# The q and k transposes of the last head group, moved from TensorE to DMAs of 16-bit planes

## Chip, cores and metric

One core of one Trainium2 chip. The metric is the device time of one execution in microseconds (us). TensorE is called PE, VectorE DVE, ScalarE ACT, GpSimd POOL and SyncE SP, as in the rows of the profile.

## What is computed

One decoder layer on 256 tokens of width 2048, all in float32. An RMS norm of x feeds one projection, which gives q, k and v of 16 heads of 128 and three gates. Heads 0 to 3 attend by stick breaking, 4 to 9 by a softmax with a bias by distance, 10 to 15 by a dilated softmax with a bias. q and k of heads 4 to 15 are normalised per row first:

```
proj = h @ w_in
qn = rmsnorm(q[:, H_A:], q_gain[:, None, :])
kn = rmsnorm(k[:, H_A:], k_gain[:, None, :])
l = einsum('bhqd,bhkd->bhqk', qn, kn) * scale + bias      # then a masked softmax, times v
merged = sum over branches of gates * (o_branch @ w_branch)
x = x + merged @ w_out
x = x + (silu(gate(h2)) * up(h2)) @ w_down                # h2: second RMS norm
```

The scores need q and k with the head dimension on the 128 partitions; the projection leaves them with the tokens there. So every 128x128 block of q and k is transposed once.

## The kernel before, in words

**Weights.** Every weight block comes in float32 from SP's DMA queue as 128x1024. ACT rounds it to a high part (`w_hi`, line 108), DVE subtracts to get the low part (`w_lo`, line 108), and PE forms three products of 128x512 for each 128 rows (lines 170 to 172). `parts` does this for one block, with five buffers each for `w_hi` and `w_lo`. Two column blocks at a time go through one Strassen step (`project_pair`), called a unit here. A unit has 22 calls of `parts`, the last four of them ahead for the next unit (`begin_pair`). Sums of two blocks are called `u`.

**Units.** Their order in the first phase is v of group 0, a gate, q and k of groups 0 and 1 (`qk`), v of groups 1 and 2, q and k of groups 2 and 3, then v of group 3 with a gate ("vg"), and five units of two gates each. A group is four heads; group 3 is the last.

**Side work.** Generators hold the work beside the products. `stages` goes one step forward after each weight split, `slow_stages` after every second one. `rows_to_columns(3)` runs in `stages` during the unit "vg": it scales the four 128x512 tiles `sbs` (q of token tiles 0 and 1, k of 0 and 1), takes their sums of squares on ACT (line 729), works out `rr` on DVE and ACT (lines 177 to 186), multiplies each tile by it on DVE (line 739), transposes it on PE in four 128x128 pieces (`transpose4`, line 192), and takes the result out of PSUM: k by an ACT copy (line 745), q by a DVE product with the gains in reversed order (line 748). The attention of group 3 is queued in `slow_stages` after "vg", behind that of group 2.

**What follows "vg" on ACT.** v is scaled out of PSUM (line 798), the gate goes through a sigmoid (line 772, with a load of another function table), then come the splits of the first gate unit and the copies of its partial sums (`snapshot`, line 308), and beside them the softmax of group 2 (line 693, again with a table load).

**Order.** The instructions of each engine are put in order by a planner that plays the program through with its own durations; an instruction written earlier goes first among those that are ready. `keep_in_program_order` only pins an instruction behind the one written before it on its engine. On the chip each engine takes its own list in that order. `half_kb` hands out one of 12 scratch tiles of 128x512.

**The method itself is in the kernel already.** `to_a`, in the feed-forward phase, splits a tile into its 16-bit halves on ACT (line 998), transposes the halves by a DMA issued from ACT (line 1001) and joins them on ACT (line 1008); there the issue is one step behind the split, and the join at least six steps behind the last issue.

Of the kernel before, what the change touches and what calls it, by code (L numbers as in the profile page):

```python
# [11 lines left out]
U16 = mybir.dt.uint16  # L12
# [6 lines left out]
P = 128  # L19
D = 2048  # L20
S = 256
NT = S // P
KT = D // P
HD = 128
H_A, H_B, H_C = 4, 6, 6
# [30 lines left out]
def hybrid_block(ctx: ExitStack, tc: tile.TileContext, x, w_in, w_branch, w_out, w_gu, w_down, rel_bias,  # L56
                 onehot, extra, across, factors, out):
    nc = tc.nc
# [32 lines left out]
    def half_kb(dt=F32):  # L91

        return scratch.tile([P, NB], dt, name="sc")
# [80 lines left out]
    def rsqrt_mean(dst, ss, n, cols):  # L174

        v = small.tile([P, cols], F32, name=f"rs_v{cols}")
        nc.vector.tensor_scalar(v, ss, 1.0 / n, EPS, op0=ALU.mult, op1=ALU.add)
        y = small.tile([P, cols], F32, name=f"rs_y{cols}")
        nc.scalar.activation(y, v, AF.Ln)
        nc.scalar.activation(y, y, AF.Exp, scale=-0.5)  # L180
        t = small.tile([P, cols], F32, name=f"rs_t{cols}")
        for it in range(2):
            nc.vector.tensor_mul(t, y, y)
            nc.vector.tensor_mul(t, t, v)
            nc.vector.tensor_scalar(t, t, -0.5, 1.5, op0=ALU.mult, op1=ALU.add)
            nc.vector.tensor_mul(dst if it else y, y, t)

    def transpose4(src):

        pt = tr.tile([P, 4, P], F32, name="tr")  # L190
        for i in range(4):
            nc.tensor.transpose(pt[:, i, :], src[:, i * P:(i + 1) * P], ident)  # L192
        return pt


    class Columns:

# [203 lines left out]
    h = Columns(p1, "h", KT)  # L401
    hs = Both(p1, h, WC)
# [32 lines left out]
    gq = consts.tile([P, H_SOFT], F32, name="gq")  # L435
# [181 lines left out]
    def backwards(a):  # L617


        return a[..., ::-1]  # L620
# [97 lines left out]
    def rows_to_columns(g, sbs, dst):  # L718
        for i in (0, 2, 3):
            tc.keep_in_program_order(nc.scalar.activation(sbs[i], sbs[i], AF.Copy, scale=rstd[:, i % NT:i % NT + 1]))  # L720
            if i != 2:
                yield
        if g:
            ss = pa.tile([P, 4 * NT * 2], F32, name="ss", bufs=1)
            for i, sb in enumerate(sbs):
                junk = half_kb()
                for hd in range(4):
                    cols = slice(hd * HD, (hd + 1) * HD)
                    tc.keep_in_program_order(nc.scalar.activation(junk[:, cols], sb[:, cols], AF.Square,
                                                                  accum_out=ss[:, 4 * i + hd:4 * i + hd + 1]))  # L730
                    if hd % 2:
                        yield
            rr = pa.tile([P, 4 * NT * 2], F32, name="rr", bufs=1)
            rsqrt_mean(rr, ss, HD, 4 * NT * 2)
            yield
        for i, sb in enumerate(sbs):
            if g:
                sb3 = sb.rearrange("p (h d) -> p h d", h=4)
                nc.vector.tensor_mul(sb3, sb3, rr[:, 4 * i:4 * i + 4, None].to_broadcast([P, 4, HD]))
            yield  # L740
            j, t = divmod(i, NT)
            pt = transpose4(sb)
            d = dst[j][:, :, t * P:(t + 1) * P]
            if j:
                nc.scalar.copy(d, pt)
            elif g:
                hs = 4 * g - H_A
                nc.vector.tensor_mul(d, backwards(pt), gq[:, hs:hs + 4, None].to_broadcast([P, 4, P]))
            else:
                nc.scalar.activation(d, pt, AF.Copy, scale=SCALE)  # L750
        yield

    def attention(g, qT, kT, v):
        biases = []
# [50 lines left out]
    def keep_qk(g, q0, q1, k0, k1):  # L805
        sbs = [q0, half_kb(), k0, k1]
        nc.scalar.activation(sbs[1], q1, AF.Copy, scale=rstd[:, 1:2])
        heads["qk", g] = qkT = [pa.tile([P, 4, S], F32, name=f"{n}T") for n in "qk"]
        if g:
            stages.append(rows_to_columns(g, sbs, qkT))  # L810
        else:
            slow_stages.append(rows_to_columns(g, sbs, qkT))
            attend(g)
# [161 lines left out]
    a = Chunks(None, "a", NF // 4, WD, False)  # L975
# [231 lines left out]
```

## Time and profile before

| | |
|---|---|
| median of 3 runs | 1344.98 us (1343.92 to 1347.02) |
| the profiled execution | 1344.12 us, its span 1342.4 us, 1.7 us outside the span |
| granted clock of PE | 1.00 (2.4 GHz) |
| busy | PE 99%, DVE 86%, ACT 68%, POOL 9% of the span |

A busy share is an average over the whole span. What a change of 20 us in one place is worth is read from that place: the order of time on PE, ACT and DVE there, and the spare time between the end of a weight split and its first product. An ACT row of two or more instructions gives the time from the start of the first to the end of the last; consecutive ones overlap by about 0.1 us.

### The profile page before, as it was taken

The numbers are of one execution on the slowest core, as the hardware profiler recorded it, in microseconds if no ns is written. First come the engines' busy times: TensorE is split into PE (matmuls) and PEld (weight loads), VectorE is DVE, ScalarE is ACT, GpSimd is POOL, SyncE is SP. The second block draws the span as 40 slices with busy tenths as digits, with TensorE's granted clock in tenths as the row PEclk, the third lists the DMA queues.
The fourth block names the chain that finished last, engine by engine and source line by source line (L and its number), as shares of the span: only waits on it lengthen the run. The fifth ranks groups of instructions, "written<-read, shape, count | busy, mean of one in ns | idle before, by whom it ended". The sixth has DMA issues, their size and how long they took to land.

```text
span 1342.4 us, 17715 instructions
## 1 busy us (share of the span) xinstructions
PE 1333.9 (99%) x6266; PEld 1165.2 (87%) x6266; DVE 1154.9 (86%) x1239; ACT 917.4 (68%) x1175; POOL 118.0 (9%) x180
## 2 busy tenths in 40 slices
PE   9999999999999999999999999999999999999998
PEld 6888888888888888888888888888888888888887
DVE  7988898988889996876689999999999997996785
ACT  7786967888776775445567778777877876664453
POOL 1100010101110112100100000001000001000000
PEclk9999999999999999999999999999999999999999
DMA  9987877888788878977788989899999987787652
GB/s 361 305 282 248 268 208 246 269 255 244 250 276 278 268 241 286 309 232 223 238 325 258 269 250 282 222 263 302 289 281 284 245 240 254 251 307 239 204 186 96
DMA packets 117200, 346.83 MB, mean 258 GB/s; under 512 B 32576, under 2 KB 34296, under 8 KB 117112
## 3 DMA queue, kind: packets, MB, share of 16 engines
q1 hardware_dynamic: 76872, 277.45, 59.6%
q0 software_dynamic: 17824, 61.90, 19.7%
q10 hardware_dynamic: 22416, 6.36, 2.8%
q8 instruction: 49, 0.80, 0.2%
q14 instruction: 39, 0.32, 0.1%
HBM read 293.21 MB, written 14.70 MB: 229 GB/s over the span
## 4 chain that ended last, share of the span: by engine, by line
PE 96%; DVE 2%; ACT 1%; issue 0%; DMA 0%; SPq 0%; DVEq 0%; ACTq 0%
PE qs L171 12%; PE qs L170 12%; PE qs L172 12%; PE ps L171 12%; PE ps L172 12%; PE ps L170 12%; PE z L170 4%; PE z L171 4%; PE z L172 4%; PE v L171 2%; PE v L172 2%; PE v L170 2%; PE tr L172 1%; PE tr L170 1%; PE tr L171 1%; PE tr L192 1%
## 5 line engine op out<-in xcount | busy, mean ns | idle before, releaser
L108 DVE TENSOR_TENSOR w_lo<-w_raw,w_hi 128x1024 fp32r<-128x1024 f32 x318 | 386.9, 1221 | 86.2 <-ACT w_hi L108 84.6
L108 ACT CAST w_hi<-w_raw 128x1024 fp32r<-128x1024 f32 x318 | 331.8, 1048 | 142.9 <-PE qs L172 49.3
L108 ACT CAST w_hi<-g_raw 128x1024 fp32r<-128x1024 f32 x200 | 207.5, 1049 | 131.8 <-PE qs L172 37.1
L108 DVE TENSOR_TENSOR w_lo<-g_raw,w_hi 128x1024 fp32r<-128x1024 f32 x200 | 238.7, 1221 | 29.6 <-ACT w_hi L108 28.0
L108 ACT CAST w_hi<-u 128x1024 fp32r<-128x1024 f32 x150 | 155.4, 1047 | 79.7 <-PE ps L172 20.7
L108 DVE TENSOR_TENSOR w_lo<-u,w_hi 128x1024 fp32r<-128x1024 f32 x150 | 180.6, 1221 | 32.9 <-ACT w_hi L108 29.9
L171 PE MATMUL qs<-w_lo,h_hi 128*128 128x512 f32 x348 | 132.7, 381 | 0.0
L172 PE MATMUL qs<-w_hi,h_lo 128*128 128x512 f32 x348 | 132.2, 380 | 0.0
L171 PE MATMUL ps<-w_lo,h_hi 128*128 128x512 f32 x336 | 128.1, 382 | 0.2 <-DVE w_lo L108 0.2
L172 PE MATMUL ps<-w_hi,h_lo 128*128 128x512 f32 x336 | 127.5, 380 | 0.1
L170 PE MATMUL qs<-w_hi,h_hi 128*128 128x512 f32 x348 | 125.0, 382 | 0.0
L170 PE MATMUL ps<-w_hi,h_hi 128*128 128x512 f32 x336 | 121.1, 382 | 0.0
L170 PEld LDWEIGHTS qs<-w_hi,h_hi 128*128 128x128 f32 x348 | 65.9, 189 | 9.4 <-ACT sc L308 0.4
L171 PEld LDWEIGHTS qs<-w_lo,h_hi 128*128 128x128 f32 x348 | 65.9, 189 | 9.1
L172 PEld LDWEIGHTS qs<-w_hi,h_lo 128*128 128x128 f32 x348 | 65.9, 189 | 9.1
L172 PEld LDWEIGHTS ps<-w_hi,h_lo 128*128 128x128 f32 x336 | 63.6, 189 | 9.7 <-DVE h_lo L108 1.1
L171 PEld LDWEIGHTS ps<-w_lo,h_hi 128*128 128x128 f32 x336 | 63.6, 189 | 9.6 <-DVE w_lo L108 1.1
L170 PEld LDWEIGHTS ps<-w_hi,h_hi 128*128 128x128 f32 x336 | 63.4, 190 | 8.9 <-ACT h_hi L108 0.3
L366 POOL DMA_DIRECT2D u<-g_raw x44 | 38.2, 868 | 363.6 <-DVE w_lo L108 252.5
L324 DVE TENSOR_TENSOR u<-g_raw 128x1024 f32<-128x1024 f32 x44 | 53.6, 1220 | 7.7 <-DMA g_raw<-in_w_gu 5.8
L313 DVE TENSOR_TENSOR u<-u,g_raw 128x1024 f32<-128x1024 f32 x44 | 51.8, 1218 | 0.0
L171 PE MATMUL z<-w_lo,h_hi 128*128 128x512 f32 x104 | 39.5, 380 | 0.0
(400 smaller groups left out, 2956.5 us busy)
## 6 DMA issues: line engine op xcount, KB each, us to landing
w_raw<-in_w_in SPq DMA_DIRECT2D x104, 512.0 KB, 6.8
g_raw<-in_w_in SPq DMA_DIRECT2D x88, 512.0 KB, 6.5
g_raw<-in_w_gu SPq DMA_DIRECT2D x88, 512.0 KB, 6.2
w_raw<-in_w_gu SPq DMA_DIRECT2D x88, 512.0 KB, 7.4
w_raw<-in_w_down SPq DMA_DIRECT2D x64, 512.0 KB, 4.3
u<-g_raw POOLq DMA_DIRECT2D x44, 512.0 KB, 6.9
w_raw<-in_w_branch SPq DMA_DIRECT2D x32, 512.0 KB, 4.9
w_raw<-in_w_out SPq DMA_DIRECT2D x32, 512.0 KB, 4.4
```

The source lines that it names most:

```text
L108: for op in nc.scalar.copy(hi, src), nc.vector.tensor_sub(lo, src, hi.bitcast(F32)):
L170: nc.tensor.matmul(ps, ah, wh, start=start, stop=False, **how)
L171: nc.tensor.matmul(ps, ah, wl, start=False, stop=False, **how)
L172: nc.tensor.matmul(ps, al, wh, start=False, stop=stop, **how)
L192: nc.tensor.transpose(pt[:, i, :], src[:, i * P:(i + 1) * P], ident)
L313: tc.keep_in_program_order(nc.vector.tensor_add(d, d, a))
L324: nc.vector.tensor_add(d, a, b)
L366: nc.gpsimd.dma_start(d, a, accum_op=ALU.add)
```

## The change

For group 3 alone the transposes leave PE. After its product with `rr`, each of the four tiles is copied on ACT into a plane of low and a plane of high 16-bit halves (`send_across`), and a DMA issued from ACT writes the transposed planes back over the tile. Three empty steps later ACT joins the halves (`take_across`), one tile a step: k straight into `kT`, q into the tile that held its halves, from which DVE multiplies it by the gains into `qT` (`by_gain`, the old line 748 in a function of its own).

```
+    def send_across(src, turned):
+        halves = half_kb()
+        tc.keep_in_program_order(nc.scalar.copy(halves.bitcast(U16).rearrange("p (h n) -> p h n", h=2),
+                                                src.bitcast(U16).rearrange("p (n h) -> p h n", h=2)))
+        nc.scalar.dma_start_transpose(turned.bitcast(U16).rearrange("p (e q) -> p e q", e=8), halves.bitcast(U16))
+        return halves
+
+    def take_across(dst, turned):
+        tc.keep_in_program_order(nc.scalar.copy(dst, turned.bitcast(U16).rearrange("p (h k q) -> p h k q", h=2, k=4)))
+
+    def words(a):
+        return a.bitcast(U16).rearrange("p (k q h) -> p h k q", k=4, h=2)
...
+        back = []
         for i, sb in enumerate(sbs):
             if g:
                 sb3 = sb.rearrange("p (h d) -> p h d", h=4)
                 nc.vector.tensor_mul(sb3, sb3, rr[:, 4 * i:4 * i + 4, None].to_broadcast([P, 4, HD]))
             yield
+            if g == 3:
+                back.append(send_across(sb, sb))
+                continue
             j, t = divmod(i, NT)
             pt = transpose4(sb)
             d = dst[j][:, :, t * P:(t + 1) * P]
             if j:
                 nc.scalar.copy(d, pt)
             elif g:
-                hs = 4 * g - H_A
-                nc.vector.tensor_mul(d, backwards(pt), gq[:, hs:hs + 4, None].to_broadcast([P, 4, P]))
+                by_gain(d, g, pt)
             else:
                 nc.scalar.activation(d, pt, AF.Copy, scale=SCALE)
-        yield
+        for _ in range(3 if back else 1):
+            yield
+        for i, own in enumerate(back):
+            yield
+            j, t = divmod(i, NT)
+            if j:
+                take_across(dst[j].bitcast(U16).rearrange("p k (q h) -> p h k q", h=2)[:, :, :, t * P:(t + 1) * P], sbs[i])
+            else:
+                take_across(words(own), sbs[i])
+                by_gain(dst[j][:, :, t * P:(t + 1) * P], g, own.rearrange("p (k q) -> p k q", k=4))
+
+    def by_gain(d, g, src):
+        hs = 4 * g - H_A
+        nc.vector.tensor_mul(d, backwards(src), gq[:, hs:hs + 4, None].to_broadcast([P, 4, P]))
```

## Rows read from the trace of the kernel before

**Rows 1.** The page's part 1: busy time of each engine.

```profile
PE 1333.9 (99%) x6266; PEld 1165.2 (87%) x6266; DVE 1154.9 (86%) x1239; ACT 917.4 (68%) x1175; POOL 118.0 (9%) x180
```

**Rows 2.** Waits of PE: total us, times, longest; a row of four.

```profile
PE qs L171 <- DVE w_lo L108: 1.1, 2, 0.8
```

**Rows 3.** The chain that ended last: start us, us, what.

```profile
322.96 0.44 PE tr L192 x4
...
361.24 0.86 PE att L676 x4
```

**Rows 4.** Timeline of ACT after `rr` is known: start us, us, what [idle before].

```profile
305.81 1.05 ACT L108 CAST w_hi<-g_raw 128x1024 fp32r<-128x1024 f32 x1 [1.54 <-PE qs L172]
307.53 0.69 ACT L798 ACTIVATE v<-qs,rstd 128x512 f32<-128x512 f32 x1 [0.68 <-PE qs L172]
308.61 1.05 ACT L108 CAST w_hi<-u 128x1024 fp32r<-128x1024 f32 x1 [0.39 <-DVE sc L739]
...
312.22 1.03 ACT L108 CAST w_hi<-u 128x1024 fp32r<-128x1024 f32 x1
...
314.24 1.05 ACT L108 CAST w_hi<-w_raw 128x1024 fp32r<-128x1024 f32 x1
...
320.16 0.58 ACT L745 COPY kT<-tr 128x512 f32<-128x512 f32 x1
320.63 2.00 ACT L108 CAST w_hi<-u 128x1024 fp32r<-128x1024 f32 x2
```

**Rows 5.** Timeline of DVE in the same stretch.

```profile
306.10 2.49 DVE L739 TENSOR_TENSOR sc<-sc,rr 128x512 f32<-128x512 f32 x4
...
313.28 1.23 DVE L108 TENSOR_TENSOR w_lo<-u,w_hi 128x1024 fp32r<-128x1024 f32 x1 [0.23 <-ACT w_hi L108]
```

**Rows 6.** Timeline of PE: the first products with those splits.

```profile
316.01 0.46 PE L170 MATMUL qs<-w_hi,h_hi 128*128 128x512 f32 x1
316.31 0.38 PE L171 MATMUL qs<-w_lo,b_shi 128*128 128x512 f32 x1
...
323.45 0.38 PE L170 MATMUL ps<-w_hi,b_shi 128*128 128x512 f32 x1
```

**Rows 7.** Busy us and instructions of the engines by stretch.

```profile
316.00:327.00 11.00, 11.00 (x59) 9.48 (x58) 10.03 (x14) 10.97 (x20) 1.79 (x2) 1.00 0.75 226
327.00:348.00 21.00, 21.00 (x106) 18.53 (x105) 17.78 (x20) 12.48 (x16) 0.00 (x0) 1.00 0.77 276
```

**Rows 8.** The tiles `halves` and `turned` of `to_a`: duration ns min/median/max.

```profile
L998 ACT COPY halves<-sc x20: 1043/1045/1058, 733.3 to 1084.8; 128x1024 uint16<-128x1024 uint16 x20
L1001 ACTq DMA_TRANSPOSE turned<-halves x20: 1247/1284/1541, 734.4 to 1085.9; - x20
L1008 ACT COPY sc<-turned x20: 1333/1352/1360, 755.8 to 1106.7; 128x1024 uint16<-128x1024 uint16 x20
DMA to landing us min/median/max: 5.2/6.7/9.6
```

**Rows 9.** Waits of ACT that nothing but an issue explains.

```profile
ACT sc L308 <- issue: 14.3, 10, 1.7
ACT w_hi L108 <- issue: 2.5, 2, 1.4
```

**Rows 10.** Timeline of ACT in the first round of `to_a`.

```profile
734.36 1.36 ACTq L1001 DMA_TRANSPOSE turned<-halves  x1
735.17 1.04 ACT L998 COPY halves<-sc 128x1024 uint16<-128x1024 uint16 x1
736.25 1.44 ACTq L1001 DMA_TRANSPOSE turned<-halves  x1
737.78 0.59 ACT L308 COPY sc<-z 128x512 f32<-128x512 f32 x1 [1.57 <-issue]
...
755.84 2.56 ACT L1008 COPY sc<-turned 128x1024 uint16<-128x1024 uint16 x2
```

**Rows 11.** The page's part 3: the queue of ACT's DMAs.

```profile
q10 hardware_dynamic: 22416, 6.36, 2.8%
```

## The prediction

> **What bounds the kernel now.** I read the page's busy times first. PE is busy 1333.9 of the 1342.4 us of the span [rows 1]. Busy matmuls could hide waits, so I read PE's waits next: four rows, of which one lies inside the stream of weight products, 1.1 us in two pieces [rows 2]. In the stretch of the change it is busy for 11.00 of 11.00 us and for 21.00 of 21.00 us [rows 7]. So PE's list of products is the kernel: an edit gains what it takes off PE, and loses what it makes PE wait. Nothing else can be gained, and the list stays full only as long as ACT and DVE deliver the split weights in time.
>
> Next I read the place of the change in order of time. `rr` is finished on DVE shortly before 306.1, when the four products with it run, 0.62 us apart [rows 5]. At that moment ACT ends the last split of the unit "vg" (305.81 + 1.05 = 306.86), and from there to 327 it has two pauses, 0.68 and 0.39 us [rows 4]; between 316 and 327 it is busy 10.97 of 11.00 us. Only after that it has room: 12.48 of 21.00 us, so 8.5 us free [rows 7]. The spare time of the weights is at its smallest here. The second `u` split (312.22) ends at 313.25, its low part on DVE at 313.28 + 1.23 = 314.51, and PE reads it at 316.31: 1.8 us. The next split (314.24) ends at 315.29 and PE reads it at 316.01: 0.7 us. The `u` split of 320.63 ends about 321.6 (two in 2.00 us, so 0.95 us from one to the next) and PE reads it at 323.45: 1.8 us [rows 4 to 6].
>
> **What the change removes.** 16 transposes on PE: four take 0.44 us [rows 3], so 4 x 0.44 = 1.76 us, and 1344.1 - 1.8 = 1342.3 us if nothing else moved. Two evictions of k on ACT at 0.47 us from their start to the next start [rows 4]: 0.95 us. The two q products stay on DVE; reading the joined tile in place of PSUM is not shown here. The nearest row is the product with `rr`, which reads that kind of tile at the same size and takes 2.49 us for four, 0.62 apiece [rows 5]; the q product from PSUM is of the same kind of size, so I take no difference, and 0.1 us either way twice is no part of the sum.
>
> **What it adds.** Four copies into halves on ACT: 1.045 us each, 0.95 from start to start like the splits [rows 8, 4], 3.8 us. Four joins: 1.352 us each [rows 8], less the 0.1 us overlap 1.25, so 5.0 us. Four DMA issues on ACT's queue, 1.25 to 1.54 us each [rows 8]. What an issue costs ACT depends on what stands around it. In `to_a` the first of a pair lies behind a copy and costs nothing (734.36, while the next copy starts on time at 735.17); the second follows its own copy and leaves ACT idle for 1.57 us [rows 10]. All 20 issues left it idle for 14.3 + 2.5 = 16.8 us [rows 9], 0.84 us each. Bounds for four: 0, and 4 x 1.43 = 5.7 us when each directly follows its own copy (1.43 is 14.3 over 10). In `send_across` copy and issue are written one behind the other with no step between, which is nearer to the bad case than `to_a` is, but four copies can pass the issues one after the other, so I take the mean: 3.4 us.
>
> So the sending takes 3.8 + 3.4 = 7.2 us of ACT (bounds 3.8 and 9.5). It can start at 306.8 and was written before the scaling of v, the sigmoid and the splits of the next unit, so it goes ahead of them in ACT's list. The two pauses take 1.1 us of it; 6.1 us are left over (2.7 to 8.4). What is queued behind: v's scaling (whose PSUM bank a later partial sum needs), both `u` splits, the sigmoid with its table, the first partial-sum copy, the next splits; for all of the splits PE waits. The `u` split of 312.22 has 1.8 us to spare, so PE waits 6.1 - 1.8 = 4.3 us (bounds 0.9 and 6.6). The 0.7 us of the split at 314.24 I don't take: that one product stands early between two others and can be listed later.
>
> The joins need the DMAs landed, 6.7 us after the issue in `to_a` [rows 8], so from about 315 on. Their cost on PE lies between nothing and 5.0 - 0.95 = 4.05 us. Nothing, if ACT does them in the 8.5 us free after 327 [rows 7]; nothing needs them sooner, for the scores of group 3 start at 361.24 [rows 3]. All of it, if they stand in ACT's list ahead of the `u` split of 320.63. The nearest row is the join in `to_a`, 755.84 against an issue at 736.25, 19.6 us later [rows 10]; I take nothing, and keep 4.05 for the range.
>
> The last four of the transposes taken away stand at 322.96 [rows 3], before PE reads the `u` split of 320.63 at 323.45 [rows 6]; the other twelve are earlier. With the splits late PE only comes to its wait sooner, and I credit none of the 1.8 us. The added transfers have room: the 20 transposes and a few small DMAs of that queue took 2.8% of 16 engines' span [rows 11], under 37.6 us, under 1.9 us each; four are 7.5 us in a stretch where the DMA engines are 75 and 77% busy [rows 7], 0.25 x 11 + 0.23 x 21 = 7.6 us free from 316 to 348.
>
> **The sum.** 1344.1 + 4.3 = 1348.4 us against the profiled execution. The median of the runs, 1345.0, is 0.9 us above that execution, so I forecast 1349 us. A measurement of this kernel tells about 0.2%, 2.7 us, from no change; 4.3 us is just beyond.
>
> **Rivals.** *All hidden.* The planner puts the four copies and issues between the splits so that none of those is late: 1344.1 - 1.8 = 1342.3, or 1343 against the median. For it: taken over 306.9 to 348 ACT has 1.1 + 8.5 = 9.6 us free, and needs 7.2 + 4.05 = 11.3 more, of which a lead of splits could lend the rest. Against it: the free time comes behind the smallest spare time.
>
> *The issues cost nothing.* As the first issue of each pair in `to_a` [rows 10], all four stand behind running work. Then only the copies count: 3.8 - 1.1 - 1.8 = 0.9 us of wait, against half of the 16 transposes, which stand behind 316.31, the last four at 322.96 [rows 3] (0.9 us): 1344 us, no change, and this ends on the other side of my forecast. It decides as soon as the issues leave under 1.5 us of ACT idle. The Trainium skill (DMA: Bandwidth & Descriptors, "Issuing engines are not separate DMA queues") says that the time on the sequencer to start a DMA is usually small relative to the DMA itself, and in "Anatomy of one DMA" gives about 50 ns of dispatch; by that the four issues would cost 0.2 us and this rival would hold. The trace disagrees for these DMAs: 1.25 to 1.54 us on ACT's queue against 6.7 us to landing [rows 8], and half of them leave ACT idle.
>
> *The joins come too early.* They stand in the list ahead of the `u` splits: 6.1 + 4.05 - 1.8 = 8.3 us of wait, 1352.4 us; if they stand there before the DMA has landed (up to 9.6 us in place of 6.7 [rows 8]), up to 2.9 us more, 1355.3. For it: they are written before those splits and are ready about 315 to 321. Against it: three empty steps and one more per tile, and the row of 755.84.
>
> *Scratch tiles.* Four more of 12 are held from the copy to the join. If a partial sum's copy has to wait for one, PE waits for its PSUM bank. At 312 I count four tiles, four halves, three results of "vg" and one gate, which makes 12; with one more it would cost about one landing, 6.7 us, and end near the rival before. I count it with that one.
>
> **How the numbers follow.** Forecast 0.45 (1345.5 to 1351, 0.05 of it within 0.2%); all hidden 0.18; issues free 0.18; joins early or tiles short 0.15; a gain over 0.2% 0.04, because PE has only 1.8 us to give up and a few tenths of waits. Slower by over 0.2%: 0.40 + 0.15 = 0.55; within 0.2%: 0.05 + 0.18 + 0.18 = 0.41; faster 0.04. The range reaches from 1342.5 (all hidden, against the profiled execution) to 1353.5 (joins early, with the 0.9 us of the median); the forecast's own range is 1345.5 to 1351.
>
> **What will show it.** No transposes of line 192 between 306 and 324 any more (16 fewer on PE). On ACT four copies into halves from about 306.9, and idle time put down to an issue: 3.4 us by my sum, none by the second rival. Splits of `u` of the next unit some 6 us later than 308.61 and 312.22 against the products. New waits of PE on `w_hi` or `w_lo` at about 316, 4.3 us in all. Joins after 327 by my sum, between 315 and 321 by the third rival. The prediction is wrong if PE's waits stay near zero: then ACT's list was mixed so that the splits kept their spare time.

## The result and the profile after

The changed kernel takes 1357.23 us (median of 4 runs, 1355.11 to 1358.06), the kernel before 1346.00 beside it (4 runs): a ratio of 1.0084, 95% interval 1.0069 to 1.0099. It is 11 us slower, 8 us above my forecast and 3.7 us beyond the end of my range. The profiled execution spans 1353.4 us against 1342.4, 11.0 us more, and the reading below is of that difference. Line numbers have shifted by the added functions: line 739 is now 753, 798 is 827, 772 is 801, 308 is 321, 693 is 706.

The page's part 1 after the change, and the queue of ACT's DMAs from its part 3 (packets, MB, share of 16 engines):

```profile
PE 1336.5 (99%) x6250; PEld 1164.9 (86%) x6250; DVE 1154.6 (85%) x1239; ACT 925.0 (68%) x1181; POOL 118.2 (9%) x180
...
q10 hardware_dynamic: 26640, 7.41, 3.2%
```

Beside [rows 1] the 16 transposes are gone (6266 to 6250), and yet PE is busy 2.6 us longer, and idle for 8.4 us more. Beside [rows 11] there are 4224 more packets, 1056 for each tile of 256 KB, so about 250 bytes each.

The waits of PE after the change:

```profile
PE qs L170 <- ACT w_hi L108: 8.7, 2, 8.5
```

This row did not exist before [rows 2]. The stretches of [rows 7] after the change, and two pieces of 2 us out of them:

```profile
316.00:327.00 11.00, 2.34 (x8) 1.32 (x7) 2.08 (x3) 7.46 (x9) 1.15 (x2) 0.76 0.91 185
327.00:348.00 21.00, 21.00 (x93) 18.22 (x93) 16.96 (x22) 18.50 (x28) 1.74 (x2) 0.88 0.69 198
...
322.00:324.00 2.00, 0.00 (x0) 0.00 (x0) 0.38 (x1) 1.74 (x2) 0.00 (x0) 0.50 1.09 298
...
332.00:334.00 2.00, 2.00 (x12) 1.79 (x11) 0.58 (x1) 2.00 (x3) 0.00 (x0) 1.00 0.15 59
```

PE, busy for 11.00 of 11.00 us before, is busy for 2.34. And the granted clock, 1.00 throughout before, is 0.50 (1.2 GHz in place of 2.4) from 322 until shortly before 332. PE's timeline shows both:

```profile
316.75 0.38 PE L172 MATMUL qs<-w_hi,b_slo 128*128 128x512 f32 x1
325.64 0.80 PE L170 MATMUL qs<-w_hi,b_shi 128*128 128x512 f32 x1 [8.51 <-ACT w_hi L108]
326.58 0.80 PE L170 MATMUL qs<-w_hi,h_hi 128*128 128x512 f32 x1 [0.15 <-ACT w_hi L108]
327.17 0.63 PE L171 MATMUL qs<-w_lo,b_shi 128*128 128x512 f32 x1
327.60 0.63 PE L172 MATMUL qs<-w_hi,b_slo 128*128 128x512 f32 x1
```

PE stands from 317.13 to 325.64. From 327.17 on the products start 0.43 us apart, and from 332.75 on 0.22 apart again. The 13 products between 325.64 and 331.87 take 6.23 us, less the wait of 0.15, where 13 at 0.216 take 2.81: 3.3 us more, 0.5 of it in the first two products after the wait. So 8.66 us of wait (8.51 + 0.15) + 3.3 us at the lower clock - 1.76 us of transposes = 10.2 of the 11.0 us. I can't place the other 0.8.

ACT's timeline says why the split was late; it answers to [rows 4]:

```profile
305.37 0.51 ACT L706 ACTIVATE p<-p,sm_st 128x256 f32<-128x256 f32 x1 [0.78 <-DVE sm_st L700]
...
308.08 1.05 ACT L108 CAST w_hi<-g_raw 128x1024 fp32r<-128x1024 f32 x1
...
309.62 1.98 ACT L198 COPY sc<-sc 128x1024 uint16<-128x1024 uint16 x2
310.68 1.33 ACTq L200 DMA_TRANSPOSE sc<-sc  x1
...
312.04 5.44 ACTq L200 DMA_TRANSPOSE sc<-sc  x1
312.44 1.99 ACT L198 COPY sc<-sc 128x1024 uint16<-128x1024 uint16 x2
317.53 0.72 ACT L827 ACTIVATE v<-sc,rstd 128x512 f32<-128x512 f32 x1 [3.09 <-issue]
317.66 3.13 ACTq L200 DMA_TRANSPOSE sc<-sc  x1
...
320.89 1.33 ACTq L200 DMA_TRANSPOSE sc<-sc  x1
322.26 1.33 ACT L204 COPY sc<-sc 128x1024 uint16<-128x1024 uint16 x1 [1.98 <-issue]
...
324.08 0.56 ACT L321 COPY sc<-ps 128x512 f32<-128x512 f32 x1
324.54 1.04 ACT L108 CAST w_hi<-u 128x1024 fp32r<-128x1024 f32 x1
```

The second `u` split starts at 324.54, 12.3 us later than before (312.22). Two of the four issues stay on the queue for 5.44 and 3.13 us, where the slowest in `to_a` took 1.54 [rows 8], and ACT idles for 3.09 + 1.98 = 5.07 us behind them. The rest of the 12.3 us is order. A softmax of group 2, with a copy of `o_raw` behind it, has moved ahead of "vg"'s last split (308.08 in place of 305.81: 2.3 us), the four copies stand ahead (3.8 us, less the 1.1 us of pauses), one join does (1.2 us), and so do the second scaling of v and the `snapshot` (1.1 us), which before came behind that split. 5.1 + 2.3 + 2.7 + 1.2 + 1.1 = 12.4 us.

What kept the issues is in the DMA view of three consecutive windows, 312.04 to 314, 314 to 316 and 316 to 317.5:

```profile
q0 software_dynamic: 51, 0.21, 53.2%
q1 hardware_dynamic: 121, 0.41, 51.9%
q10 hardware_dynamic: 22, 0.01, 2.2%
...
q0 software_dynamic: 88, 0.32, 81.9%
q10 hardware_dynamic: 312, 0.08, 22.9%
...
q10 hardware_dynamic: 725, 0.18, 67.4%
q0 software_dynamic: 50, 0.18, 61.6%
```

q1 holds the weight loads, q0 POOL's DMAs. Here those are two accumulating ones of 512 KB that add the blocks of the next unit, issued in the same two microseconds as the first two transposes. POOL's timeline after the change (line 373):

```profile
310.23 1.07 POOL L373 DMA_DIRECT2D g_raw<-g_raw  x1 [5.51 <-issue]
311.64 0.87 POOL L373 DMA_DIRECT2D g_raw<-g_raw  x1 [0.34 <-ACT sc L198]
```

The 22 + 312 + 725 = 1059 packets of ACT's queue in these windows are about those of the first transpose (1056); it lands at 317.6, and the second issue ends at 317.48. From 314 to 316 the 88 packets of q0 take 81.9% of 16 engines for 2 us, so 0.30 us each, and 312 of the transpose's go between them: 47 beside 46 of q0 in the first of the two microseconds, 265 beside 42 in the second, where q0's share has fallen from 96.6 to 67.2%.

### The profile page after: what moved, and what is told of

Same layout as the page of the kernel before. It is cut to its first block, busy times and chain, and to the rows that moved or that the text cites. A ratio compares the mean times of both kernels' runs of the same rounds, so it can differ in the third digit from the quotient of the medians.

```text
span 1353.4 us, 17704 instructions
## 1 busy us (share of the span) xinstructions
PE 1336.5 (99%) x6250; PEld 1164.9 (86%) x6250; DVE 1154.6 (85%) x1239; ACT 925.0 (68%) x1181; POOL 118.2 (9%) x180
## 4 chain that ended last, share of the span: by engine, by line
PE 73%; DVE 1%; ACT 1%; issue 0%; ACTq 0%; DVEq 0%
PE qs L171 9%; PE qs L170 9%; PE qs L172 9%; PE ps L170 8%; PE ps L171 8%; PE ps L172 8%; PE z L170 4%; PE z L171 4%; PE z L172 4%; PE v L170 2%; PE v L171 2%; PE v L172 2%; PE tr L172 1%; PE tr L170 1%; PE tr L171 1%; ACT w_hi L108 1%
## 5 line engine op out<-in xcount | busy, mean ns | idle before, releaser
L170 PE MATMUL qs<-w_hi,b_shi 128*128 128x512 f32 x80 | 31.6, 395 | 8.6 <-ACT w_hi L108 8.5
```

The costliest lines, as they stand in the source:

```text
L170: nc.tensor.matmul(ps, ah, wh, start=start, stop=False, **how)
```

## The experiments

Theory 1: the issues take long beside the accumulating DMAs and hold ACT's list. Theory 2: it is ACT's added work, copies and joins ahead of the splits, whatever the DMAs do.

**The DMAs left out** (`copies_no_dma`). Copies and joins stay; the joins read the halves as they are, so q and k of group 3 are not transposed.

```
-        nc.scalar.dma_start_transpose(turned.bitcast(U16)..., halves.bitcast(U16))
...
-                take_across(dst[j]..., sbs[i])
+                take_across(dst[j]..., own)
```

> The changed kernel without its four DMAs: the copies into halves and the joins stay, the joins read the untransposed halves (q and k of group 3 are not transposed, so that part of the computation is left out). Theory 1, the issues: ACT's idle time put down to an issue (3.09 + 1.98 us in the changed kernel) is what made the second u split of the next unit late; without it PE's wait at that place falls from 8.5 to under 4 us, PE keeps its full clock, and the time is 1343 to 1349 us, about 8 to 14 us under the changed kernel. Theory 2, the work: the 3.8 us of copies and 5.0 us of joins are enough; PE still waits 7 us or more there and the time stays above 1352 us.

1351.08 us, ratio 1.0043 (1.0028 to 1.0058): between the two. PE waits:

```profile
PE qs L170 <- ACT w_hi L108: 2.8, 1, 2.8
```

Without a transfer to wait for, three joins stand among the splits (314.47, 316.62, 321.44), and the clock is 0.50 from 324 to 328. So joins alone can cost some us where they come early, and 6 us of the 11 go with the DMAs. The planner has also put ACT's list in another order without them (the second `u` split at 315.68 stands ahead of the sigmoid), so the 6 us need not be the issues alone.

**The sum of the next unit on DVE** (`sum_on_dve`): no accumulating DMAs beside the transposes.

```
-            ps, ahead = project_pair(*pair_of(kind, what), ahead, nxt, others is in_turn)
+            ps, ahead = project_pair(*pair_of(kind, what), ahead, nxt, others is in_turn and not (kind == "gates" and what[0] == chunks[2]))
```

> The changed kernel, but in the one unit after vg the sum of b12 and b22 is made by two DVE additions (2.4 us of DVE) in place of two accumulating DMAs of POOL. Theory 1a, the transposes share the DMA engines with the two accumulating transfers issued at 310.2 and 311.6 and so drain slowly: the second and third issue on ACT fall from 5.44 and 3.13 to under 1.8 us each, PE's wait falls to 2 to 5 us, the time to 1345 to 1351 us. Theory 1b, more than one transpose in flight on that queue is slow by itself: the second and third issue stay above 3 us and the time above 1353 us.

1355.34 us, 1.0072 (1.0057 to 1.0087). Here two parts of theory 1 were set against each other: 1a, that the issues are long beside the accumulating DMAs, and 1b, that they are long with more than one transpose in flight anyhow. The issues fall to 1.33, 1.88, 1.25 and 1.28 us, as 1a wants and against 1b. But the time hardly moves, outside the range of 1a: three joins now stand ahead of the second `u` split, which comes at 323.37, and PE waits 7.5 us for `w_hi`. One cause had taken the other's place; the two had to be taken apart.

**The whole crossing in the next unit** (`across_later`): copies in its steps 5 to 8, each DMA one step behind, joins in steps 11 to 14.

```
+            stages.append(across_later(3, heads["rows", 3], heads["qk", 3]))
```

> The same four transposes by DMA, but moved from the end of the unit vg into the next one: copies in steps 5 to 8, each DMA one step behind its copy, joins in steps 11 to 14, behind the dense stretch of ACT. Both theories, if the place is the cause: no wait of PE over 1 us at the u splits, time 1342 to 1346 us, within 0.2% of before. If four transposes by DMA cost this wherever they stand: two issues above 3 us again, a PE wait of 4 us or more, and over 1349 us.

1360.14 us, 1.0120 (1.0102 to 1.0139), the slowest of those run more than once. The stretch that lost time before is clean (PE 11.00 of 11.00 us from 316 to 327), and the loss appears where the crossing went. ACT's timeline:

```profile
335.01 6.09 ACTq L203 DMA_TRANSPOSE sc<-sc  x1
...
341.20 0.58 ACT L323 COPY sc<-ps 128x512 f32<-128x512 f32 x1 [3.87 <-issue]
348.43 1.33 ACT L206 COPY kT<-sc 128x1024 uint16<-128x1024 uint16 x1 [5.69 <-DMA sc<-sc]
```

One issue is long again (I had expected two, or none), and now a join waits 5.69 us for its tile at the head of ACT's list, with the splits behind it; PE waits 8.7 us, 3.5 for the copy at 341.20 and 5.2 for splits. Beside this issue stand weight loads, and there turns by packet do not explain it: from 336 to 340 only 44 packets of the loads and 275 of the transposes go, 0.24 MB in 4 us, where the loads alone moved 0.82 MB in 2 us in the next run. Why both are slow there I did not find.

**Eight transposes of no use in the kernel before** (`probe_issues`): four behind the accumulating DMAs of one gate unit ("loaded"), four in another gate unit away from them ("quiet").

```
+    def four_transposes(src):
+        for _ in range(4):
+            tc.keep_in_program_order(nc.scalar.dma_start_transpose(
+                half_kb().bitcast(U16).rearrange("p (e q) -> p e q", e=8), src.bitcast(U16)))
```

> The kernel before with eight more DMA transposes whose results nobody reads, four in a row right behind the accumulating DMAs of one gate unit, four in a row in the next gate unit where no accumulating DMA is under way. Theory 1a (sharing with the accumulating transfers): beside them the second to fourth issue take 2 us or more each, over 8 us in all; away from them all stay under 1.8 us. Theory 1b (more than one in flight): both groups show issues over 3 us from the second on. Neither: all eight 1.2 to 1.6 us.

1363.36 us (one run). Both groups are slow, so my picture of the quiet one was wrong. That is near to what 1b expected; but in `sum_on_dve`, with more than one transpose in flight, the issues stayed under 1.9 us. The timeline of ACT, and the DMA view from 435 to 437:

```profile
367.69 8.14 ACTq L332 DMA_TRANSPOSE sc<-sc  x3
...
429.40 13.28 ACTq L332 DMA_TRANSPOSE sc<-sc  x4
```

```profile
q1 hardware_dynamic: 216, 0.79, 96.1%
q10 hardware_dynamic: 216, 0.06, 12.2%
```

Beside the quiet group weight loads fill the queue. In those 2 us, 216 of their packets go and 216 of the transposes', one for one; but theirs carry 3.7 KB each (0.79 MB) and take 0.14 us (96.1% of 16 engines), the transposes' carry about 0.25 KB. From 441 to 443, with no load in the queue, 2145 packets of q10 go. The Trainium skill (DMA: Bandwidth & Descriptors, "Queues, rings and completion order") says that each DMA engine goes round the queues that have work, one packet at a time; 216 to 216 agrees. So it is not the accumulating DMAs alone: the weight loads slow the small packets too. Beside POOL's queue, where that is full, it is one for one as well (47 to 46 above), and its packets take twice as long.

**The joins later, alone and with the sum on DVE** (`joins_late`, `joins_late_sum_on_dve`). Copies and DMAs stay in place, the joins go to steps 11 to 14 of the next unit. The two differ only in the line of `sum_on_dve`.

```
-        for _ in range(3 if back else 1):
+        heads["back", g] = back, sbs, dst
+        yield
+
+    def join_later(g, first):
...
+            stages.append(join_later(3, 11))
```

> The changed kernel with its copies and DMAs where they are, but with the four joins moved into steps 11 to 14 of the next unit, behind the late u split. Theory 1, the issues on ACT's queue (5.44 and 3.13 us in the changed kernel, because the transposes' small packets take turns with those of the accumulating DMAs): they stay, only one join of 1.2 us leaves the way of the u split; PE still waits 6 to 8 us there, time 1352 to 1357 us. Theory 2, the joins: PE's wait falls under 4 us and the time under 1350 us.

> As the kernel before it in this list, and the sum of b12 and b22 in the unit after vg made by DVE in place of the two accumulating DMAs. ACT's list is the same in both. Theory 1: the issues fall to under 2 us each as they did with the joins early, the u split comes some 4 us sooner, PE waits 2 to 4 us, time 1346 to 1350 us. If the difference to the kernel before it is under 2 us, the long issues are not what ACT's late split costs.

1357.89 us (1.0092, 1.0072 to 1.0112) and 1348.37 us (10 runs; 1.0024, 1.0014 to 1.0033): 9.5 us apart. The four runs of the first lie between 1353.96 and 1360.37, and the two profiled executions are 7.1 us apart. Down to the second `u` split the two lists of ACT are the same. With the accumulating DMAs, ACT's timeline and the wait of PE:

```profile
312.08 5.71 ACTq L200 DMA_TRANSPOSE sc<-sc  x1
...
317.84 0.72 ACT L832 ACTIVATE v<-sc,rstd 128x512 f32<-128x512 f32 x1 [3.36 <-issue]
317.98 3.96 ACTq L200 DMA_TRANSPOSE sc<-sc  x1
...
323.36 0.72 ACT L806 ACTIVATE sc<-sc,rstd 128x512 f32<-128x512 f32 x1 [2.76 <-issue]
...
324.45 1.04 ACT L108 CAST w_hi<-u 128x1024 fp32r<-128x1024 f32 x1
...
PE qs L170 <- ACT w_hi L108: 8.5, 2, 8.4
```

And without them:

```profile
311.90 2.12 ACTq L200 DMA_TRANSPOSE sc<-sc  x1
...
314.19 0.72 ACT L832 ACTIVATE v<-sc,rstd 128x512 f32<-128x512 f32 x1
314.20 1.25 ACTq L200 DMA_TRANSPOSE sc<-sc  x1
...
317.96 1.04 ACT L108 CAST w_hi<-u 128x1024 fp32r<-128x1024 f32 x1
...
PE qs L170 <- ACT w_hi L108: 2.6, 2, 2.1
```

The idle time behind issues, 3.36 + 2.76 = 6.1 us, is gone. The split comes at 317.96 in place of 324.45, and PE waits 2.6 us in place of 8.5. This is the pair that shows theory 1: the long issues come from transposes and accumulating DMAs together, and the idle time behind them makes this split 6.5 us later. The next run keeps the accumulating DMAs and has no transposes, and loses nothing, so the accumulating DMAs by themselves do not cost this.

**Joins late and no DMAs** (`no_dma_joins_late`): both edits together, what the copies cost by themselves.

> The four copies stay, the DMAs are left out, the joins stand in steps 11 to 14 of the next unit and read the untransposed halves (q and k of group 3 are not transposed, that part of the computation is left out). This is the price of the 3.8 us of copies alone. Theory 1: PE waits under 2 us, time 1343 to 1347 us, at least 4 us under the run without DMA whose joins stood early (1351.1). Rival: the joins were not what that run lost by, and the time stays at 1349 or above.

1344.26 us (10 runs; 0.9996, 0.9986 to 1.0005). The split stands at 314.91, PE waits 0.9 us for `w_hi`, and the clock is 1.00 throughout. In this list the copies cost next to nothing: 0.9 us of wait, against the 1.76 us of transposes that this kernel doesn't have either. But part of that is order: the planner put the sigmoid and its table load (2.6 us) behind the second `u` split, and the changed kernel has them ahead. In that order, and with no idle time behind an issue, the split stands at 317.96 and PE waits 2.6 us (`joins_late_sum_on_dve`). Against `copies_no_dma` the joins' place is worth 6.8 us.

**One transpose at a time** (`spaced`): one every five steps over two units, each join eight steps behind its DMA, the attention of group 3 started behind the last.

```
+            if r == 1 and i < 4:
+                turn_across(own[i], sbs[i])
+            i, r = divmod(n - 9, 5)
```

> The same four transposes by DMA, one every five steps over the next two units, each join eight steps behind its DMA, and the attention of group 3 begun behind the last join. Theory 1: alone in its queue each issue takes 1.2 to 2 us even beside other transfers, no wait of PE over 1 us, time 1342 to 1346 us: the saved transposes (1.8 us) and nothing more. Rival: each transpose by DMA costs ACT so much in these units that splits come late wherever it stands: PE waits over 3 us in all, time above 1348 us.

1354.66 us, 1.0072 (1.0056 to 1.0089), a miss. No issue is long (1.25 to 2.19 us), but:

```profile
344.82 1.35 ACT L206 COPY sc<-sc 128x1024 uint16<-128x1024 uint16 x1 [4.50 <-DMA sc<-sc]
```

That tile's DMA was issued at 329.75 and lands 15.0 us later. In that time 1056 packets of q10 and 1216 of the weight loads went, again about one for one. So the wait moved from the issue to the join, and with it the splits: PE waits 3.5 us for `w_lo` until 349.74, and its clock is 0.50 from 350 to 354.

**Issued from SP** (`from_sync_joins_late`, and `from_sync_sum_on_dve` with the sum on DVE): as the two runs with late joins, with the issues off ACT's queue.

```
-        nc.scalar.dma_start_transpose(...)
+        nc.sync.dma_start_transpose(...)
```

> As joins_late (joins in steps 11 to 14 of the unit after "vg", the accumulating DMAs left in), but the four transposes are issued from SP's queue, so no issue can hold ACT. Theory 1 (the cost is ACT's idle time behind issues that take long): the second u split ends near 315 as without any transpose, PE's wait at it falls from 8.5 us to about 1, the granted clock stays at 1.00, and the time is 1344 to 1347.5 us against 1357.9. Theory 2 (the cost is that the transposes' packets slow the accumulating DMAs and the weight loads, whoever issues them): the u split still comes late, for its sum lands late, and the time stays above 1352 us. A third outcome: the issues take as long on SP's queue and keep the weight loads behind them; then PE waits on a w_hi or w_lo whose w_raw landed late, and the time is above 1350 us.

> As the run before, and the sum of the unit after "vg" on DVE, so there are no accumulating DMAs in that stretch. Theory 1: nothing is left of the cost but what the joins and DVE's added sums take, 1343.5 to 1347 us; against the kernel before it can gain at most the 1.76 us of the 16 transposes. If the issues on SP hold the weight loads, 1347 us or more with PE waiting on w_hi or w_lo behind a late w_raw.

1356.93 us (6 runs; 1.0079, 1.0065 to 1.0093) and 1356.28 us (5 runs; 1.0079, 1.0064 to 1.0095). The profiled execution of the first was its slowest (1368.40), so I read the second: the view by line of its issues, the longest wait of SP and the first row of PE's waits.

```profile
L200 SPq DMA_TRANSPOSE sc<-sc x4: 1231/1239/1349, 296.6 to 308.0; - x4
...
DMA to landing us min/median/max: 2.7/2.7/2.8
```

```profile
SPq L200 <- ACT sc L198: 25.0, 1, 25.0
...
PE qs L170 <- ACT w_hi L108: 6.6, 3, 3.2
```

My third outcome, but not for its reason. No issue is long. The first one stands on SP for 25.0 us until its halves are written, and the weight loads, which SP's queue issues in order, stand behind it. The queues run empty (26 packets from 290 to 295), and then PE waits for splits of weights that land late. The same emptiness gives the transposes an undisturbed landing of 2.7 us, against 5.2 to 9.9 in the changed kernel.

## Why the prediction was wrong

The step that failed is the lateness of the second `u` split: 6.1 us in the sum, 12.3 measured. In it the issues were too small and three pieces of ACT's order were missing; behind it the price of a wait left out the clock. The issues and the joins were taken apart by experiments; the rest of the order is read from the trace.

**PE's list is the kernel, and the 16 transposes are 1.76 us:** right. An edit that made PE wait cost what it made it wait, and more.

**Copies, 3.8 us:** the duration is right (1.98 for two). They start at 309.62 and not at 306.9, behind the softmax. What they cost depends on the rest of the list: in `no_dma_joins_late` the split is 2.7 us late and PE waits 0.9, in the order with the sigmoid ahead it is 5.7 us late and PE waits 2.6 (`joins_late_sum_on_dve`).

**Issues: "so I take the mean: 3.4 us".** This term failed. They held ACT's queue for 11.2 us (1.33 + 5.44 + 3.13 + 1.33), and 5.07 us of it was idle time in front of the late split. My row for the price, `to_a`, showed issues of at most 1.54 us. The idle time still lies inside my bounds of 0 to 5.7, but I derived these from how copies and issues alternate; it was the DMA queues that set the length. The step behind it, "The added transfers have room", is where that went unseen. I compared busy time with free time (7.5 against 7.6 us). But a transpose doesn't wait for free time and then take it: its 1056 small packets take turns with whatever else is queued. The row to look for was that POOL issues two accumulating DMAs at this very place, in the kernel before too:

```profile
308.21 0.86 POOL L360 DMA_DIRECT2D g_raw<-g_raw  x1 [20.11 <-DMA g_raw<-in_w_in]
310.63 0.85 POOL L360 DMA_DIRECT2D g_raw<-g_raw  x1 [1.55 <-DVE sc L387]
```

With them the idle time is 5.1 to 6.1 us, without them nothing (`joins_late_sum_on_dve`): the mean of 3.4 is right in neither case. The rival with free issues fell with it. The Trainium skill's rule that stood beside that rival (DMA: Bandwidth & Descriptors, "Issuing engines are not separate DMA queues"; the time to start a DMA is usually small relative to the DMA itself) does not hold for these transposes: 5.44 us on the queue against 9.9 to landing for the second one, and 1.24 against 2.7 where they ran alone, on SP's queue. The 50 ns that my prediction takes from the same page stand there for DMAs issued by GpSimd, and these come from ACT.

**6.1 us late at the second `u` split:** 12.3. What I had too small are the issues (by 1.7 us); what I had at nothing are one join (1.2), the softmax (2.3) and v and `snapshot` (1.1). So 4.6 of the 6.2 us are the order of ACT's list, in which I had counted nothing but my own additions. The softmax's place alone costs nothing: `across_later` has it too, and PE is busy for 11.00 of 11.00 us. Of the 12.3 us, 8.7 became wait; 3.6 were covered, where I had 1.8.

**Joins absorbed after 327:** three of four were; one stood ahead of the split. The rival "joins come too early" names a real mechanism, which `sum_on_dve` and `copies_no_dma` show; in the changed kernel it is 1.2 us of the lateness. It was priced up to 1355.3 us, and the end of my range, 1353.5, leaves that out. Of a wait for scratch tiles no run shows anything.

**The clock:** in none of my cases, so a term put at nothing without a reason. A wait of 4.3 us was priced as 4.3 us; this one of 8.5 us cost 3.3 more, at 1.2 GHz, and a wait of 2.1 us in `joins_late_sum_on_dve` was followed by 1.2 GHz too.

**The sum:** 1348.4 us for the profiled execution, which took 1355.1. Of the 6.7 us between them 4.4 are wait (8.7 in place of 4.3), 3.3 the lower clock and 0.8 unplaced, less the 1.76 of transposes, of which I had credited none.

With the long issues and the early joins both gone, `joins_late_sum_on_dve` takes 1348.37 us, near my 1349, but that is luck. Its split is 5.7 us late against my 6.1, yet with no idle time behind issues (mine 3.4), and with the softmax (2.1), v and `snapshot` (1.1) that I did not have; its wait is 2.6 us and not 4.3, and the clock adds to it. It also has the free issues of my rival, which put that at 1344. What was right is the chain: work ahead of the `u` split on ACT makes PE wait. What stays open is what ends a long issue inside the queue. In the changed kernel and `joins_late` the second ended when 1059 and 1047 packets of q10 had gone, in the two runs with the sum on DVE after 555 and 534; so it goes with the packets of the transposes before it, but by which rule I did not find. Also open is why the planner moved the softmax ahead. No version beats the kernel before: at most 1.76 us were to be had, under what a measurement tells.

## What to carry to other kernels

Price a DMA transpose by the queues around it, not by the same operation elsewhere in the kernel: list what the weight loads and the other engines' DMAs have in flight at its place, and count its packets against theirs. Whatever waits for it, the issuing queue, a join or the loads behind it on SP, must not stand ahead of anything that feeds PE. And where PE has under 2 us to give up and its list is full, any work put ahead of a weight split must show its spare time first; a wait long enough for the clock to fall costs more than its length.

## What the runs showed of the hardware

- A transposed tile of 256 KB moves as 1056 packets. With the queues nearly empty it lands in 2.7 us (`from_sync_sum_on_dve`); a plain DMA of 256 KB (the gate's) landed in 2.8 us in `joins_late_sum_on_dve`. Beside full queues it took 5.2 to 9.9 us in the changed kernel, 15.0 in `spaced` and up to 20.8 in `across_later`.
- The transposes' packets took turns one for one with those of a full queue, whatever their size: 216 and 216 of the weight loads in 2 us, 47 and 46 of POOL's in 1 us. From 336 to 340 in `across_later` they did not: 275 and 44, both slow.
- A transpose's issue on ACT's queue took 1.25 us at its shortest, and up to 6.09 us (`across_later`) behind unfinished transposes.
- After PE had stood still from 317.1 in the changed kernel, the granted clock was 0.91 from 320 to 322 and 0.50 from 322; in `joins_late_sum_on_dve` a wait of only 2.1 us was followed by 0.71 and 0.50 from 320 to 324. It was 1.00 again from 332 in the changed kernel, and from 326 in `joins_late_sum_on_dve`.
